# Merging the key split of the second attention, moving its weights to the queries, copying a query half on GpSimd, and four more embedding buffers

## The chip, the core and the metric

The kernel runs as one program on one core of a Trainium2 chip. The metric is the device time of one execution in microseconds; the time of a kernel is the median of its runs.

The engines, as the profile names them: PE is TensorE (matrix products; PEld is its loading of the stationary operand), DVE is VectorE, ACT is ScalarE, POOL is GpSimd, and SP is the engine that only issues DMAs here.

## What is computed

One encoder layer for two sequences (prompt and sample) of 2048 tokens and 1024 features. It normalises, projects, runs two attentions beside each other, gates each, projects back and adds; then it adds an embedding product under a second gate:

```python
h = rms_norm(x, norm_w)
q_a, k_a, v_a, g_a, q_b, k_b, v_b, g_b = jnp.split(h @ w_in, IN_SPLITS, axis=-1)
...
o_a = windowed_gqa_sink(q_a, k_a, v_a, sink_a) * jax.nn.silu(g_a)
q_b = rms_norm(q_b.reshape(b, s, B_HEADS, HEAD_DIM), q_norm_b)
k_b = rms_norm(k_b.reshape(b, s, B_HEADS, HEAD_DIM), k_norm_b)
v_b = v_b.reshape(b, s, B_HEADS, HEAD_DIM)
o_b = neighbourhood_attn(q_b, k_b, v_b, rpb_b) * jax.nn.silu(g_b)
x = x + jnp.concatenate([o_a, o_b], axis=-1) @ w_out
return x + (p @ w_ple) * jax.nn.sigmoid(x @ w_ple_gate)
```

`neighbourhood_attn` sees the tokens as a grid of 32 rows by 64 columns; a query looks at 8 rows by 16 columns of keys, with a learned bias, over 8 heads of 64 features. A score is the sum over the 64 features of query times key, so the product of the two norm weights and the scale 1/8 may stand on either side of it.

## The kernel before, in words

**Stages.** The first attention (A) with its projections comes first, until about 600 us. The second attention (B) follows, until about 1590 us. Then come three large matrix products, each done in seven products of half-size blocks (L1134). This document is about B and the turn from B to the products.

**How B is tiled.** It runs in two halves of four heads each. In a half, each sequence has 16 tiles of 128 tokens (8 grid rows by 16 grid columns), so there are 32 tiles a half and 64 in all. The first half also projects the values of all eight heads; the second has less to project. A tile f goes through `proj_b` (L705): split the input into a high and a low part, project (`project`, L451), take the root of the mean square on GpSimd, normalise keys and queries, and store keys and values. Seven tiles later its queries are used: `prep_q` (L573) and `unit_b` (L788) make the scores, `softmax` (L615), transposes, values and output of the same tile. So the last seven units run with no projection beside them.

**High and low parts.** Every operand of a matrix product is held as two numbers: a high part (rounded to the format that TensorE multiplies) and the remainder. ACT writes the high part from the PSUM bank, then DVE writes the difference.

**Keys.** TensorE transposes the four normalised key heads of a tile into one PSUM bank (L735): two pairs of heads side by side, in each pair one head in partitions 0 to 63 and one in 64 to 127. Before the change the loops at L737 and L738 go over the two pairs i and the two heads e. Each of the four turns has one ACT instruction `k1` (L745, high part, scaled by the weights `wk`) and one DVE instruction `k2` (L749, low part). They store into `big[0]` for the first pair and `big[1]` for the second. The store is strided: the key buffer runs by grid row and then grid column, and the instruction takes a tile's elements by column and then row. In the profile these instructions are "ACTIVATE big<-bank,wk" and "SCALAR_TENSOR_TENSOR big<-bank,wk,big".

**Queries.** For each of the two heads e of a pair, `prep_q` has an ACT copy of the high part (`o1`, L602), a DVE subtraction for the low part (`o2`, L604), and a DMA (`o3`, L607) that copies the high part into the other 64 partitions, since a score matmul multiplies one 128-partition stationary operand by keys that hold high and low parts in the two halves of the partitions. All of it is 64 partitions by 256 elements in B.

**Embeddings.** `embed` (L909) multiplies the embedding input by its weights in 64 groups of six matmuls with 512 columns. A group takes a PSUM bank and an `ev` buffer, ACT evicts it into the buffer (L929), and a DMA stores it to memory (`ple_d`). The buffers become free for that when the projections have ended (`no_projections`, L1018): two of the eight `wb` weight tiles give four buffers. All groups must be done before the second of the seven products, whose weights take the place of the embedding weights.

**What sets the order.** The program is recorded by a planner (`Flow`, L93). Each `op` carries an engine, an assumed duration in ns, its inputs, a priority (the lower number goes first) and the buffers it takes and frees. The planner runs these assumed times forward and writes each engine's instructions in the order that comes out; on the chip every engine then takes its instructions in that order. Embeddings have the priority 5003.5 on TensorE, so they fill what attention leaves. GpSimd's sums of weights (`combine`, L887) fill in the same way. A change of an assumed duration or an engine can therefore move instructions far from it.

Of the kernel before, what the change touches and what calls it, by code (L numbers as in the profile page):

```python
# [12 lines left out]
F32 = mybir.dt.float32  # L13
F32R = mybir.dt.float32r
# [209 lines left out]
def emit(ctx, tc, io):  # L224
# [57 lines left out]
    op = F.op  # L282
# [65 lines left out]
    big = [new([128, 4096], F32R, f"big{i}") for i in range(3)]  # L348
# [3 lines left out]
    ks_b = [big[i].rearrange("p (e r c) -> p e r c", e=2, c=64) for i in range(2)]  # L352
# [220 lines left out]
    def prep_q(f):  # L573
# [26 lines left out]
        for e in range(2):  # L600
            a, z = 64 * e, 64 - 64 * e
            o1 = op("ACT", 92 + 0.78 * w, lambda e=e, a=a: A.copy(dst_of(hi[e]()[a:a + 64]), src_of(a)), [t, first_hi], pr,  # L602
                    take=[q1[e]] if in_a else [q1[0]] if e == 0 else (), free=[bank])
            o2 = op("DVE", 85 + 1.04 * w, lambda e=e, a=a: V.tensor_tensor(  # L604
                out=dst_of(q2.t[a:a + 64, e, :w]), in0=src_of(a), in1=dst_of(hi[e]()[a:a + 64].bitcast(F32)), op=ALU.subtract),
                [o1, *out[:1]], pr, take=[q2] if e == 0 else (), free=[bank])
            o3 = dma(lambda e=e, z=z: hi[e]()[z:z + 64].bitcast(F32), lambda e=e, a=a: hi[e]()[a:a + 64].bitcast(F32), w / 4, [o1], pr)  # L607
# [97 lines left out]
    def proj_b(f, w_qk, qk_done, w_v, v_done, prios, gate):  # L705
# [31 lines left out]
        for i in range(2):  # L737
            for e in range(2):  # L738
                a, z = 64 * e, 64 - 64 * e

                def hl(i=i, e=e, a=a, z=z):
                    src = kb.t[a:a + 64, 128 * i:128 * i + 128].rearrange("p (c r) -> p c r", r=8)
                    return (src, *(ks_b[i][p:p + 64, e, 8 * b:8 * b + 8, 16 * cb:16 * cb + 16].rearrange("p r c -> p c r") for p in (a, z)))

                def k1(v=hl, a=a):  # L745
                    src, hi, _ = v()
                    A.activation(hi, src, AF.Copy, scale=wk[a:a + 64, 1:2])

                def k2(v=hl, a=a):  # L749
                    src, hi, lo = v()  # L750
# [3 lines left out]
                keys_of[f] += [o1, o2]  # L754
# [263 lines left out]
    def no_projections():  # L1018
# [275 lines left out]
```

## Time and profile before

| | |
|---|---|
| median of 3 runs | 2567.73 us (2567.34 to 2568.16) |
| the profiled execution's own time | 2568.98 us |
| its span, first to last instruction | 2566.9 us |
| mean granted TensorE clock | 0.985 |
| PE, DVE, ACT, POOL busy in the span | 96%, 69%, 61%, 46% |

The prediction quotes rows in these forms. A row of busy time has the stretch, its length, and for each engine the busy us and the number of instructions. A row of a group has the source line, engine, operation, output<-inputs, shape and count, then the busy us and the mean ns of one, then the idle time ahead of these instructions and what ended it. L215 is the helper that records every operation, so groups are told apart by the names of their buffers: `big` holds keys in both attentions, `q` the split queries, `s` scores, `p_t` probabilities, `xr` split input, `ev` embedding results, `misc` small work. A row of waits has who waited for whom, the total in us, how often, and the longest. L276 is a matrix product, L279 a transpose, L1134 one of the three large products.

### The profile page before, as it was taken

The numbers are of one execution on the slowest core, as the hardware profiler recorded it, in microseconds if no ns is written. First come the engines' busy times: TensorE is split into PE (matmuls) and PEld (weight loads), VectorE is DVE, ScalarE is ACT, GpSimd is POOL, SyncE is SP. The second block draws the span as 40 slices with busy tenths as digits, with TensorE's granted clock in tenths as the row PEclk, the third lists the DMA queues.
The fourth block names the chain that finished last, engine by engine and source line by source line (L and its number), as shares of the span: only waits on it lengthen the run. The fifth ranks groups of instructions, "written<-read, shape, count | busy, mean of one in ns | idle before, by whom it ended". The sixth has DMA issues, their size and how long they took to land. (4 is left out here: it accounts for less than half of the span.)

```text
span 2566.9 us, 39582 instructions
## 1 busy us (share of the span) xinstructions
PE 2462.5 (96%) x12468; PEld 2042.7 (80%) x12468; DVE 1769.5 (69%) x3622; ACT 1569.9 (61%) x3430; POOL 1169.9 (46%) x1537
## 2 busy tenths in 40 slices
PE   8999999999999999998989989899999999999999
PEld 6888888888787877777767778788888788888887
DVE  5888888884657565677776773477678566766765
ACT  6889889885657566677777786544443222344443
POOL 6677777765454554466666553043332000013323
PEclk9999999999999999999999999999999999999999
DMA  5634363336667666666766567866567556646654
GB/s 161 189 112 148 115 184 106 92 103 216 214 216 219 213 209 210 217 189 186 226 202 206 185 208 243 273 205 204 187 230 266 191 199 206 228 146 220 201 177 139
DMA packets 267345, 490.20 MB, mean 191 GB/s; under 512 B 28832, under 2 KB 91488, under 8 KB 257632
## 3 DMA queue, kind: packets, MB, share of 16 engines
q1 hardware_dynamic: 267136, 487.67, 59.8%
q8 instruction: 99, 1.62, 0.3%
q14 instruction: 110, 0.90, 0.1%
HBM read 340.73 MB, written 145.78 MB: 190 GB/s over the span
## 5 line engine op out<-in xcount | busy, mean ns | idle before, releaser
L276 PE MATMUL bank<-wb,xr 128*128 128x512 f32 x1536 | 399.9, 405 | 7.7 <-DVE big L215 3.1
L276 PE MATMUL bank<-wa,xr 128*128 128x512 f32 x1536 | 391.3, 400 | 6.0 <-ACT wa L215 2.9
L215 POOL TENSOR_TENSOR xr<-st,xr 128x512 fp32r<-128x512 f32 x208 | 269.4, 1297 | 225.3 <-ACT xr L215 214.7
L276 PEld LDWEIGHTS bank<-wb,xr 128*128 128x128 f32 x1536 | 285.6, 193 | 68.1 <-DVE big L215 3.8
L215 ACT ACTIVATE s<-s,nm 128x288 f32<-128x288 f32 (+6 forms) x512 | 290.0, 567 | 76.6 <-DVE nm L215 70.4
L276 PEld LDWEIGHTS bank<-wa,xr 128*128 128x128 f32 x1536 | 281.4, 190 | 63.8 <-ACT wa L215 3.6
L215 POOL TENSOR_SCALAR s<-s,rd 128x288 f32<-128x288 f32 (+6 forms) x512 | 270.4, 546 | 123.4 <-DVE rd L215 97.2
L215 DVE TENSOR_TENSOR p_t<-bank,p_t 128x512 fp32r<-128x512 f32 (+3 forms) x440 | 262.1, 625 | 52.9 <-ACT p_t L215 48.8
L215 ACT CAST p_t<-bank 128x512 fp32r<-128x512 f32 (+3 forms) x440 | 221.7, 542 | 47.1 <-PE bank L279 40.5
L279 PE MATMUL bank<-ident,s 128*128 128x128 f32 (+2 forms) x1568 | 221.2, 276 | 28.4 <-DVE big L215 12.0
L276 PE MATMUL bank<-big,q 128*128 128x288 f32 (+4 forms) x1024 | 226.7, 338 | 18.5 <-DVE p_t L215 6.2
L279 PEld LDWEIGHTS bank<-ident,s 128*128 128x128 f32 (+2 forms) x1568 | 180.1, 139 | 58.7 <-issue 10.3
L1134 PE MATMUL bank<-o,wa 128*128 128x512 f32 x912 | 209.8, 389 | 0.0
L276 PEld LDWEIGHTS bank<-big,q 128*128 128x128 f32 x1024 | 160.2, 191 | 57.3 <-DVE p_t L215 15.9
L215 DVE SCALAR_TENSOR_TENSOR big<-bank,wk,big 64x128 fp32r<-64x128 f32 x320 | 137.1, 429 | 99.2 <-ACT big L215 91.6
L215 POOL TENSOR_TENSOR s<-s,q 128x512 f32<-128x512 f32 x20 | 32.2, 1614 | 376.3 <-DVE s L215 375.6
L1134 PEld LDWEIGHTS bank<-o,wa 128*128 128x128 f32 x912 | 171.2, 188 | 35.5
L1134 PE MATMUL bank<-xr,wa 128*128 128x512 f32 x816 | 189.7, 392 | 4.2 <-ACT wa L215 2.3
L215 DVE TENSOR_TENSOR misc<-bank,misc 64x256 f32<-64x256 f32 (+1 forms) x256 | 141.8, 554 | 73.9 <-ACT misc L215 69.3
L215 POOL TENSOR_TENSOR y<-vr,half_neg 128x8 f32<-128x8 f32 (+1 forms) x128 | 185.5, 1449 | 8.7
L215 ACT COPY misc<-bank 64x256 f32<-64x256 f32 (+1 forms) x256 | 121.1, 473 | 103.4 <-PE bank L276 89.6
L1134 PEld LDWEIGHTS bank<-xr,wa 128*128 128x128 f32 x816 | 154.3, 189 | 37.1 <-ACT wa L215 2.8
(182 smaller groups left out, 4790.1 us busy)
## 6 DMA issues: line engine op xcount, KB each, us to landing
st<-x_b SPq DMA_DIRECT2D x128, 256.0 KB
vw<-v_d SPq DMA_DIRECT2D x101, 256.0 KB
st<-x_a SPq DMA_DIRECT2D x64, 256.0 KB
st<-x_n SPq DMA_DIRECT2D x64, 256.0 KB
v_d<-sq SPq DMA_DIRECT2D x64, 256.0 KB
ple_d<-ev SPq DMA_DIRECT2D x64, 256.0 KB
st<-ple_d SPq DMA_DIRECT2D x64, 256.0 KB
v_d<-sq SPq DMA_DIRECT2D x96, 128.0 KB
```

Source lines behind the costliest of these rows:

```text
L215: return lambda *a, **k: self.tc.keep_in_program_order(f(*a, **k))
L276: pinned(nc.tensor.matmul(out, lhsT, rhs, start=start, stop=stop))
L279: pinned(nc.tensor.transpose(out, in_, ident[:in_.shape[0], :in_.shape[0]]))
L1134: pinned(nc.tensor.matmul(st[0].t, w[k][:, x, c:c + 128], o[y][:, k], start=first and k == 0 and j == 0, stop=k == 3 and j == 2, skip_grou ...
```

## The change

1. The two key buffers become the two halves of one tile, `pair`. `k1` and `k2` now cover both pairs of heads: two instructions of each kind per tile of 64 partitions by 256 elements, where there were four of 64 by 128. They no longer apply weights. The durations assumed are 560 and 540 ns, where 398 and 375 stood.
2. The weights go to the queries of B: the ACT copy becomes an ACT scaling (`ACTIVATE q<-bank,wk`), the DVE subtraction a scaled subtraction (`SCALAR_TENSOR_TENSOR`). In the first attention nothing changes.
3. In B the copy of the high half into the other partitions is no DMA on SP's queue any more, but a GpSimd copy of 64x256, assumed at 480 ns. These are 128 instructions.
4. Four `wb` tiles instead of two become embedding buffers: eight buffers for four.

```diff
-    big = [new([128, 4096], F32R, f"big{i}") for i in range(3)]
+    pair = new([128, 2, 4096], F32R, "pair")
+    big = [pair[:, 0], pair[:, 1], new([128, 4096], F32R, "big2")]
...
-    ks_b = [big[i].rearrange("p (e r c) -> p e r c", e=2, c=64) for i in range(2)]
+    ks_b = pair.rearrange("p i (e r c) -> p i e r c", e=2, c=64)
...
+            def high(e=e, a=a):
+                if in_a:
+                    A.copy(dst_of(hi[e]()[a:a + 64]), src_of(a))
+                else:
+                    A.activation(hi[e]()[a:a + 64], src_of(a), AF.Copy, scale=wk[a:a + 64, 1:2])
+
+            def rest(e=e, a=a):
+                out, high = dst_of(q2.t[a:a + 64, e, :w]), dst_of(hi[e]()[a:a + 64].bitcast(F32))
+                if in_a:
+                    V.tensor_tensor(out=out, in0=src_of(a), in1=high, op=ALU.subtract)
+                else:
+                    V.scalar_tensor_tensor(out=out, in0=src_of(a), scalar=wk[a:a + 64, 1:2], in1=high, op0=ALU.mult, op1=ALU.subtract)
...
-            o3 = dma(lambda e=e, z=z: hi[e]()[z:z + 64].bitcast(F32), lambda e=e, a=a: hi[e]()[a:a + 64].bitcast(F32), w / 4, [o1], pr)
+            if in_a:
+                o3 = dma(lambda e=e, z=z: hi[e]()[z:z + 64].bitcast(F32), lambda e=e, a=a: hi[e]()[a:a + 64].bitcast(F32), w / 4, [o1], pr)
+            else:
+                o3 = op("POOL", 480, lambda e=e, a=a, z=z: G.tensor_copy(out=hi[e]()[z:z + 64], in_=hi[e]()[a:a + 64].bitcast(F32)), [o1], pr)
...
-        for i in range(2):
-            for e in range(2):
-                a, z = 64 * e, 64 - 64 * e
...
-                    A.activation(hi, src, AF.Copy, scale=wk[a:a + 64, 1:2])
...
-                    V.scalar_tensor_tensor(out=lo, in0=src, scalar=wk[a:a + 64, 1:2], in1=hi.bitcast(F32), op0=ALU.mult, op1=ALU.subtract)
-                o1 = op("ACT", 398, k1, [kp], pr, free=[kb])
-                o2 = op("DVE", 375, k2, [o1], pr, free=[kb])
...
+        for e in range(2):
+            a, z = 64 * e, 64 - 64 * e
+
+            def hl(e=e, a=a, z=z):
+                src = kb.t[a:a + 64, :256].rearrange("p (i c r) -> p i c r", i=2, r=8)
+                return (src, *(ks_b[p:p + 64, :, e, 8 * b:8 * b + 8, 16 * cb:16 * cb + 16].rearrange("p i r c -> p i c r") for p in (a, z)))
...
+                A.copy(hi, src)
...
+                V.tensor_tensor(out=lo, in0=src, in1=hi.bitcast(F32), op=ALU.subtract)
+            o1 = op("ACT", 560, k1, [kp], pr, free=[kb])
+            o2 = op("DVE", 540, k2, [o1], pr, free=[kb])
...
-        for j in range(2):
+        for j in range(4):
             t = new([128, 2, 512], F32, f"wb{j}", f"ev{j}")
             give(ev_pool, [t[:, 0], t[:, 1]])
```

The order in which instructions stand moves with it. The first place is ACT's queue in the second half of B, at the split of one tile's keys. Before, `big_178` and `big_179` are the two key buffers, `q_182` queries, `s` with `den` an exponential:

```order
L215 ACTIVATE big_178<-bank_159,wk 64x16x8 x2
L215 COPY misc<-bank_154 64x512
L215 CAST p_t<-bank_156 96x3x128
L215 ACTIVATE big_179<-bank_159,wk 64x16x8 x2
L215 CAST p_t<-bank_160 96x3x128
L215 CAST p_t<-bank_154 96x3x128
L215 ACTIVATE s_169,den<-s_169,nm 128x384
```

A place of the same kind in the changed program, where `pair` holds both key buffers:

```order
L215 ACTIVATE q_181<-bank_156,wk 64x256 x2
L215 ACTIVATE s_162,den<-s_162,nm 128x288
L215 CAST pair<-bank_159 64x2x16x8 x2
L215 ACTIVATE s_164,den<-s_164,nm 128x384
L215 ACTIVATE s_165,den<-s_165,nm 128x384
```

Four key instructions of a bank have become two, and the queries' copies carry `wk`.

The second place is GpSimd's queue in the second half of B. `s` with `rd` are the four divisions of a unit's softmax, `xr` the low part of a tile's input, `vr` and `y` the root. Before:

```order
L215 TENSOR_TENSOR xr_173<-st_175,xr_173 128x512
L215 TENSOR_SCALAR s_165<-s_165,rd 128x384
L215 TENSOR_SCALAR s_166<-s_166,rd 128x384
L215 TENSOR_SCALAR s_163<-s_163,rd 128x384
L215 TENSOR_SCALAR s_168<-s_168,rd 128x384
L215 TENSOR_SCALAR s_169<-s_169,rd 128x288
```

In the changed program (`CAST q_181<-q_181` is the new copy):

```order
L215 TENSOR_SCALAR s_164<-s_164,rd 128x512
L215 CAST q_181<-q_181 64x256
L215 TENSOR_SCALAR s_165<-s_165,rd 128x360
L215 TENSOR_SCALAR s_166<-s_166,rd 128x360
L215 TENSOR_SCALAR s_167<-s_167,rd 128x360
L215 TENSOR_SCALAR s_168<-s_168,rd 128x360
L215 CAST q_181<-q_181 64x256 x3
```

The copies stand between the divisions of one unit and the next.

The third place is SP's queue at the end of the embeddings. `ple_d<-ev` stores an embedding result; `big_178<-sums`, `big_179<-sums` and `a_15910<-w_g_c` load weights of the large products. Before:

```order
L215 DMA big_178<-sums_115 128x512 x3
L215 DMA ple_d_96<-ev_15031 128x512 x2
L215 DMA ple_d_96<-ev_15032 128x512 x2
L215 DMA big_178<-sums_115 128x512
L215 DMA big_179<-sums_115 128x512 x2
L215 DMA ple_d_97<-ev_15031 128x512 x2
L215 DMA ple_d_97<-ev_15032 128x512 x2
L215 DMA big_179<-sums_115 128x512 x2
```

In the changed program the stores of the last embeddings (`ple_d_98`) stand there, `pair<-sums` and `wa<-w_g_c` being loads of product weights:

```order
L215 DMA ple_d_98<-ev_14813 128x512 x2
L215 DMA ple_d_98<-ev_14814 128x512 x2
L215 DMA pair<-sums_115 128x512
L215 DMA ple_d_98<-ev_14815 128x512 x2
L215 DMA ple_d_98<-ev_14816 128x512 x2
L215 DMA pair<-sums_115 128x512 x4
L215 DMA wa_135<-w_g_c 128x512
```

All but one of the weight loads have moved behind the last store. On TensorE, 243 embedding matmuls stood before the first large product and 141 behind its first 48 matmuls; now 150 stand before it and 234 behind.

More of the change, by code (lines that the diff above doesn't have):

```diff
@@ L601, in prep_q @@
             a, z = 64 * e, 64 - 64 * e
-            o1 = op("ACT", 92 + 0.78 * w, lambda e=e, a=a: A.copy(dst_of(hi[e]()[a:a + 64]), src_of(a)), [t, first_hi], pr,
-                    take=[q1[e]] if in_a else [q1[0]] if e == 0 else (), free=[bank])
-            o2 = op("DVE", 85 + 1.04 * w, lambda e=e, a=a: V.tensor_tensor(
-                out=dst_of(q2.t[a:a + 64, e, :w]), in0=src_of(a), in1=dst_of(hi[e]()[a:a + 64].bitcast(F32)), op=ALU.subtract),
-                [o1, *out[:1]], pr, take=[q2] if e == 0 else (), free=[bank])
-            o3 = dma(lambda e=e, z=z: hi[e]()[z:z + 64].bitcast(F32), lambda e=e, a=a: hi[e]()[a:a + 64].bitcast(F32), w / 4, [o1], pr)
+            def high(e=e, a=a):
[9 more added lines that the diff above has]
+                    V.scalar_tensor_tensor(out=out, in0=src_of(a), scalar=wk[a:a + 64, 1:2], in1=high, op0=ALU.mult, op1=ALU.subtract)
+            o1 = op("ACT", 92 + 0.78 * w, high, [t, first_hi], pr,
+                    take=[q1[e]] if in_a else [q1[0]] if e == 0 else (), free=[bank])
+            o2 = op("DVE", 85 + 1.04 * w, rest, [o1, *out[:1]], pr, take=[q2] if e == 0 else (), free=[bank])
+            if in_a:
+                o3 = dma(lambda e=e, z=z: hi[e]()[z:z + 64].bitcast(F32), lambda e=e, a=a: hi[e]()[a:a + 64].bitcast(F32), w / 4, [o1], pr)
+            else:
+                o3 = op("POOL", 480, lambda e=e, a=a, z=z: G.tensor_copy(out=hi[e]()[z:z + 64], in_=hi[e]()[a:a + 64].bitcast(F32)), [o1], pr)
             out += [o2, o3]
@@ L736, in proj_b, with k1, k2 @@
         keys_of[f] = []
-        for i in range(2):
-            for e in range(2):
-                a, z = 64 * e, 64 - 64 * e
[L741 to L746, printed above, removed]
-                    A.activation(hi, src, AF.Copy, scale=wk[a:a + 64, 1:2])
-                def k2(v=hl, a=a):
-                    src, hi, lo = v()
-                    V.scalar_tensor_tensor(out=lo, in0=src, scalar=wk[a:a + 64, 1:2], in1=hi.bitcast(F32), op0=ALU.mult, op1=ALU.subtract)
-                o1 = op("ACT", 398, k1, [kp], pr, free=[kb])
-                o2 = op("DVE", 375, k2, [o1], pr, free=[kb])
-                keys_of[f] += [o1, o2]
+        for e in range(2):
[3 more added lines that the diff above has]
+                return (src, *(ks_b[p:p + 64, :, e, 8 * b:8 * b + 8, 16 * cb:16 * cb + 16].rearrange("p i r c -> p i c r") for p in (a, z)))
+            def k1(v=hl):
+                src, hi, _ = v()
+                A.copy(hi, src)
+            def k2(v=hl):
+                src, hi, lo = v()
+                V.tensor_tensor(out=lo, in0=src, in1=hi.bitcast(F32), op=ALU.subtract)
+            o1 = op("ACT", 560, k1, [kp], pr, free=[kb])
+            o2 = op("DVE", 540, k2, [o1], pr, free=[kb])
+            keys_of[f] += [o1, o2]
         after_pe[f] = (ops[-1], ops[-1])
@@ L813, in sc @@
                 mm(bank.t[:, :n].rearrange("p (r c) -> p r c", c=ncol), w[:, 128 * (h // 2):128 * (h // 2) + 128],
-                   ks_b[h // 2][:, h % 2, r0:r0 + nr, c0:c0 + ncol], x == 0, x == 1)
+                   ks_b[:, h // 2, h % 2, r0:r0 + nr, c0:c0 + ncol], x == 0, x == 1)
         kd = [o for g in need for o in keys_of[g]]
```

## The prediction

> **What bounds the kernel now.** I read the page first, then busy time by stage, then who waited for whom in the stages that the change touches, then the groups by shape for prices.
>
> Busy time in four stretches (start:end, length, then busy us of PE, PEld, DVE, ACT and POOL, each with its count; granted clock, DMA share, GB/s): second attention while values are still projected, second attention with less projection, its last seven units, and the turn into the three products. The fifth row is a stretch of pure products.
>
> ```profile
> 625.00:1108.00 483.00, 457.55 (x2339) 373.05 (x2338) 295.39 (x736) 303.09 (x705) 242.55 (x279) 0.99 0.69 214
> 1108.00:1495.00 387.00, 350.79 (x1815) 278.61 (x1814) 281.79 (x696) 287.96 (x669) 247.26 (x283) 0.95 0.63 199
> 1495.00:1587.00 92.00, 87.40 (x478) 72.74 (x477) 52.86 (x136) 72.26 (x166) 37.99 (x51) 0.98 0.72 225
> 1587.00:1660.00 73.00, 64.95 (x274) 52.37 (x273) 25.76 (x24) 38.35 (x64) 6.75 (x5) 0.95 0.87 292
> 2000.00:2200.00 200.00, 200.00 (x884) 165.68 (x883) 126.27 (x125) 48.05 (x42) 0.00 (x0) 1.00 0.61 207
> ```
>
> TensorE's work is the same after the change (12468 matmuls), so only its idle time can go: 25.5 us in the first row, 36.2 in the second, 4.6 in the third, 8.1 in the fourth. No other engine is full: in the second row ACT is busy 74%, DVE 73%, POOL 64%. Whatever the change frees on them counts only as far as TensorE waits for it. Whom it waits for, in each half of the stage (engine and line, waited for: us in total, times, longest):
>
> ```profile
> PE bank L279 <- DVE big L215: 8.2, 6, 3.0
> ```
>
> ```profile
> PE bank L276 <- DVE p_t L215: 6.3, 11, 1.2
> PE bank L276 <- DVE big L215: 5.2, 5, 2.4
> PE bank L279 <- DVE big L215: 4.5, 6, 1.4
> ...
> PE bank L279 <- POOL s L215: 1.9, 3, 1.0
> ```
>
> The first row is the first half (640 to 1080 us), the others the second (1080 to 1600). The largest single cause is "DVE big", the key split: 8.2 + 5.2 + 4.5 = 17.9 us. GpSimd's softmax division costs only 1.9.
>
> **The change part by part.** Prices of the key and query steps, by shape (count | busy us, mean ns | idle before); the last two rows are the same key step in the first attention, where its output lies without a stride:
>
> ```profile
> L215 ACT ACTIVATE big<-bank,wk 64x128 fp32r<-64x128 f32 x232 | 112.5, 485 | 39.3 <-PE bank L279 33.9 <-DVE qb L215 1.1 <-DVE misc L215 1.0
> L215 DVE SCALAR_TENSOR_TENSOR big<-bank,wk,big 64x128 fp32r<-64x128 f32 x232 | 103.9, 448 | 82.4 <-ACT big L215 78.1 <-PE bank L279 1.0
> L215 DVE TENSOR_TENSOR q<-bank,q 64x256 fp32r<-64x256 f32 x122 | 51.1, 419 | 1.8
> L215 ACT CAST q<-bank 64x256 fp32r<-64x256 f32 x118 | 42.8, 364 | 3.9 <-PE bank L276 1.1 <-PE bank L279 1.1
> L215 DVE TENSOR_TENSOR qb<-bank,y 128x256 f32<-128x256 f32 x57 | 23.5, 412 | 0.0
> L215 DVE SCALAR_TENSOR_TENSOR sq<-bank,rs_b,sq 128x256 fp32r<-128x256 f32 x50 | 22.9, 477 | 11.2 <-ACT sq L215 10.9
> L215 ACT ACTIVATE sq<-bank,rs_b 128x256 fp32r<-128x256 f32 x50 | 21.8, 473 | 15.4 <-PE bank L276 11.5 <-issue 2.7 <-DMA v_d<-sq 0.8
> ```
>
> ```profile
> L215 ACT ACTIVATE big<-bank,wk 64x128 fp32r<-64x128 f32 x60 | 21.7, 362 | 3.8 <-PE bank L279 3.2
> L215 DVE SCALAR_TENSOR_TENSOR big<-bank,wk,big 64x128 fp32r<-64x128 f32 x60 | 21.0, 350 | 7.0 <-ACT big L215 4.1 <-PE bank L279 1.4
> ```
>
> *Keys.* The strided store adds 485 - 362 = 123 ns on ACT and 448 - 350 = 98 on DVE for 128 elements. The merged instruction stores 256 strided elements and has no weight to apply, so it starts from the plain query rows, 364 and 419 ns. If the stride costs by instruction, it takes 487 and 517 ns; if by element, 364 + 2 x 123 = 610 and 419 + 2 x 98 = 615. I take the second, the dearer, because a doubled run doubles what is done per element. Per tile ACT gives 4 x 485 - 2 x 610 = 720 ns back, DVE 4 x 448 - 2 x 615 = 562.
> [...]
>
> *Queries.* Each half of a query tile changes from a plain copy to a scaled one: 473 - 364 = 109 ns more on ACT, 477 - 412 = 65 on DVE, twice per unit. Net per tile and unit: ACT 720 - 218 = 502 ns less, DVE 562 - 130 = 432 less; over 64, 32.1 us of ACT and 27.6 of DVE, half of each in either half of the stage. (Stride by instruction: 48 and 40.)
>
> *The copied half.* 128 DMAs leave SP's queue, 128 copies of 64x256 enter GpSimd's. The trace has no such copy; nearest are these rows. The last one is of SP's own waits in the second half:
>
> ```profile
> L215 POOL TENSOR_TENSOR misc<-misc 128x256 f32<-128x256 f32 x64 | 47.7, 745 | 131.8 <-DVE misc L215 111.8 <-issue 9.5 <-PE bank L276 8.1
> L215 POOL TENSOR_SCALAR s<-s,rd 128x512 f32<-128x512 f32 x64 | 43.2, 693 | 23.6 <-DVE rd L215 21.9 <-PE bank L276 1.6
> L215 POOL TENSOR_SCALAR s<-s,rd 128x288 f32<-128x288 f32 x60 | 29.2, 506 | 15.0 <-DVE rd L215 15.0
> ```
>
> ```profile
> SPq L215 <- ACT q L215: 27.4, 16, 3.7
> ```
>
> One input costs (693 - 506) / 224 = 0.835 ns an element, so 256 come to 506 - 32 x 0.835 = 479 ns; the two-input row, 745, is the upper bound. I take 479: 61 us over the stage, 31 in the second half, where POOL goes from 247 to 278 of 387 us. Not full, so I cost it at nothing; what hides it is that TensorE waits 1.9 us for divisions. If that cover goes, it is the first rival. SP's gain is worth nothing to the end: none of TensorE's waits above is for a DMA of queries.
>
> *What reaches the end, before the last seven units.* One tile's key chain is 4 x 485 + 4 x 448 = 3.73 us now and 2 x 610 + 2 x 615 = 2.45 then, 34% shorter; of the 17.9 us waited for it that is 6.1 us, the lower bound. The upper bound is all of DVE's 27.6 us (ACT's is larger, but DVE ends most waits). Between, by half: the first has TensorE at 95%, so I take 4 us; in the second, with 36.2 us idle, 11 of DVE's 13.8. Together 15 us.
>
> *The last seven units and the turn.* Embedding groups (six matmuls of 512 columns, one ACT copy, one store) fill TensorE there. More buffers would let more of them in, but the order shows the reverse: between the last projection and the last values 201 of their matmuls stood, now 96; before the first product 243, now 150; the other 234 follow it. A matmul of 512 columns takes 200 / 884 = 0.226 us (fifth stretch row), so 105 x 0.226 = 23.7 us of TensorE's work leaves the third stretch. ACT loses 17 evictions and 6 splits of embedding input there, 6 key instructions net:
>
> ```profile
> L215 ACT ACTIVATE ev<-bank 128x512 f32<-128x512 f32 x48 | 28.3, 596 | 15.3 <-PE bank L276 11.7 <-ACT p_t L215 1.6 <-ACT xr L215 0.9
> L215 ACT CAST xr<-st 128x512 fp32r<-128x512 f32 x126 | 77.6, 619 | 11.0 <-PE bank L276 6.8 <-DMA st<-x_b 3.2
> ```
>
> That is 17 x 0.596 + 6 x 0.619 + (8 x 0.485 - 2 x 0.610) - 6 x 0.109 = 15.9 us of 72.3. If the stretch keeps ACT's share (72.3 of 92, 79%), it shrinks to 56.4 / 0.785 = 72 us, by 20; TensorE then does the 23.7 us later at full rate: 3.7 us lost. If it keeps TensorE's share (95%), (87.4 - 23.7) / 0.95 = 67: 1.3 won. If it does not shrink at all, 23.7 lost. I take 3.7 lost.
>
> The turn now (start us, us, engine, work, idle before):
>
> ```profile
> 1606.96 26.68 PE L276 MATMUL bank<-xr,wa 128*128 128x512 f32 x117
> 1634.46 5.80 PE L276 MATMUL bank<-xr,wa 128*128 128x512 f32 x24 [0.82 <-ACT ev L215]
> 1646.33 1.22 PE L1134 MATMUL bank<-xr,big 128*128 128x512 f32 x2 [6.06 <-ACT xr L215]
> 1648.71 9.70 PE L1134 MATMUL bank<-xr,big 128*128 128x512 f32 x34 [1.16 <-DVE xr L215]
> ```
>
> A piece of the chain that ended last, from the middle of that burst (start us, us, what):
>
> ```profile
> 1624.51 0.48 issue
> 1624.99 0.60 ACT ev L215
> 1625.60 0.32 SPq L215
> 1625.92 0.05 issue
> 1625.97 4.67 DMA big<-sums
> ```
>
> Stores of embeddings and loads of product weights alternate on SP, and ACT alternates with them: an eviction stands behind the cast of a weight, which waits 4.67 us for its load, which stands behind the stores of earlier evictions. With eight buffers the order has nearly all those loads behind the last store, so the burst runs through, but the weights of the next product arrive after it: 0.7 us of stores, 4.7 of loads, 0.62 + 0.69 of split, against the 6.06 + 1.16 now. I take 1 us won (bounds: 6 won, 4 lost).
>
> Sum: -15 + 3.7 - 1 = -12.3 us. The profiled execution took 2568.98 us (span 2566.9 and 2.1 around it), 1.25 over the median 2567.73; 2568.98 - 12.3 - 1.25 = 2555.4, so 2555.
>
> **The rivals.** *GpSimd's queue inherits SP's wait.* SP waited 27.4 us in the second half for ACT's query copies, harmlessly. Now GpSimd waits for them, and behind the copies stand the next unit's four divisions, for which TensorE's transposes wait, as the order shows. If all 27.4 reach TensorE, the time is 2555 + 27 = 2582; it is slower than before once more than 12 + 5 of the 27.4 do. For it: GpSimd takes its instructions in order and is the engine that gains work. Against: the divisions themselves wait for ACT's exponentials, so part of the wait is there anyway. [...] I give 0.17.
> *TensorE's idle is not ACT's or DVE's length* but hand-over between engines, which fewer instructions leave as it is: only the 6.1 us of key waits go, the last stretch gives 3.7 back, the turn 1: 3 us won, 2564. For it: neither engine is over 74%. 0.16.
> *The last seven units do not shrink* because two units in flight set their pace and not ACT: -15 + 23.7 - 1 = 8 slower, 2575. For it: DVE is busy only 53 of 92 us there. Against: with ACT at 79%, evictions do stand in its way. 0.07.
> That the merged key tile makes a key write wait for reads of the other pair can be set aside: in the order with its waits, the new key instructions wait for their own transposes or for DVE, none for a score matmul. A merged instruction could undo its gain only above 970 ns on ACT, twice the present row.
>
> **How the numbers follow.** Forecast 0.60, rivals 0.17, 0.16, 0.07. A measurement of this kernel can tell 0.2%, 5.1 us, from no change. Faster by more than that: the forecast and a little of the second rival, 0.62; within: the rest of the second and the weak end of the first, 0.17; slower: 0.21. The forecast's own low end is 15 replaced by 27.6, so 2543, and 5 more if the turn's six go: 2538. Upwards the range takes in the second and third rivals and half of the first: 2577.
>
> **What would show it.** In the changed profile: merged key rows near 610 and 615 ns; scaled query rows near 473 and 484; the copies near 479; waits of TensorE for the key split down from 17.9 us by a third or more; POOL waits of TensorE still a few us; the last seven units near 72 us; one burst of some 234 embedding matmuls without a gap, then one gap of 6 to 9 us. Wrong would be: TensorE waits for "POOL s" of 10 us or more (first rival), second-half idle still near 36 us (second), the last units still near 92 us (third).

## The result, and the profile after

| | before | changed |
|---|---|---|
| median of 4 runs each | 2567.53 us | 2525.14 us (2524.61 to 2528.1) |
| the profiled execution's own time | 2568.98 us | 2524.61 us |
| its span | 2566.9 us | 2522.7 us |
| mean granted TensorE clock | 0.985 | 0.991 |

The ratio is 0.984, with a 95% interval from 0.9823 to 0.9857: the change gains 42 us where 12 were forecast. The sign and most prices were right; the whole gain was three to four times the forecast.

Busy time by stage. The stages are cut at the same events in both traces: the first projection of the second attention's first half, the first and the last projection of its second half, the last product with values, and the end of the second of the large products. Before, the first two of these stretches (the other two stand in the prediction, 1495 to 1587 and 1587 to 1660, a us short of the event):

```profile
542.00:1088.00 546.00, 522.16 (x2644) 426.26 (x2643) 331.84 (x823) 339.78 (x791) 277.99 (x316) 0.99 0.66 206
1088.00:1495.00 407.00, 369.03 (x1918) 294.18 (x1917) 294.96 (x735) 302.76 (x706) 258.19 (x297) 0.95 0.63 198
```

The same four stretches of the changed kernel:

```profile
542.00:1066.00 524.00, 512.50 (x2641) 423.25 (x2640) 318.04 (x757) 323.68 (x726) 302.57 (x376) 0.99 0.66 208
1066.00:1460.00 394.00, 359.12 (x1935) 288.94 (x1935) 289.14 (x685) 294.75 (x656) 284.50 (x363) 0.98 0.62 198
1460.00:1522.00 62.00, 60.06 (x359) 50.27 (x359) 47.51 (x123) 54.71 (x131) 31.39 (x48) 1.00 0.65 201
1522.00:1618.00 96.00, 91.06 (x383) 73.65 (x382) 23.34 (x21) 51.45 (x82) 12.93 (x12) 0.95 0.71 245
```

The first half became 22 us shorter (4 forecast), the second 13 (11 forecast), and the last seven units with the turn went from 166 to 158 us (2.7 us of loss forecast). In the first half TensorE does the same matmuls (the counts differ by where the cut falls), yet its busy time fell by 9.7 us beside 12.3 us of idle time. In the second half its busy time fell by 9.9 us and its idle time by only 3.1 (38.0 to 34.9), while the granted clock rose from 0.95 to 0.98.

TensorE's waits for the key split in the changed kernel, first half (one row) and second (two rows), and its waits for GpSimd's divisions in the second half (the last two rows):

```profile
PE bank L276 <- DVE pair L215: 0.7, 1, 0.7
```

```profile
PE bank L279 <- DVE pair L215: 3.1, 3, 1.4
PE bank L276 <- DVE pair L215: 2.4, 3, 1.6
PE bank L279 <- POOL s L215: 0.9, 1, 0.9
PE bank L276 <- POOL s L215: 0.3, 1, 0.3
```

The 17.9 us have become 6.2. Waits for other work of DVE grew meanwhile: in the second half those for `nm` from 6.4 to 10.7 us and those for `misc` from 5.4 to 8.1. The prices of the new instructions, from the groups by shape between 625 and 1460 us:

```profile
L215 DVE TENSOR_TENSOR pair<-bank,pair 64x256 fp32r<-64x256 f32 x116 | 72.0, 621 | 55.7 <-ACT pair L215 54.3
L215 ACT CAST pair<-bank 64x256 fp32r<-64x256 f32 x116 | 71.1, 613 | 39.4 <-PE bank L279 38.0
L215 DVE SCALAR_TENSOR_TENSOR q<-bank,wk,q 64x256 fp32r<-64x256 f32 x114 | 54.8, 481 | 1.7
L215 ACT ACTIVATE q<-bank,wk 64x256 fp32r<-64x256 f32 x114 | 52.8, 466 | 3.1 <-PE bank L279 0.7 <-PE bank L276 0.4
L215 POOL CAST q<-q 64x256 fp32r<-64x256 f32 x114 | 45.0, 395 | 27.7 <-ACT q L215 17.9 <-issue 3.9
```

The forecast prices were 615, 610, 484, 473 and 479. And TensorE's timeline at the turn:

```profile
1544.62 53.20 PE L276 MATMUL bank<-xr,wa 128*128 128x512 f32 x234
1600.87 1.22 PE L1148 MATMUL bank<-xr,pair 128*128 128x512 f32 x2 [3.04 <-ACT xr L215]
1603.25 0.80 PE L1148 MATMUL bank<-xr,pair 128*128 128x512 f32 x1 [1.16 <-DVE xr L215]
1604.78 8.13 PE L1148 MATMUL bank<-xr,pair 128*128 128x512 f32 x21 [0.74 <-ACT pair L215]
```

One unbroken burst of 234 embedding matmuls, then gaps of 4.9 us in all.

### The profile page after: what moved, and what is told of

Its sections match the earlier page's. It is cut to its first block, busy times and chain, and to the rows that moved or that the text cites. A ratio compares the mean times of both kernels' runs of the same rounds, so it can differ in the third digit from the quotient of the medians.

```text
span 2522.7 us, 39235 instructions
## 1 busy us (share of the span) xinstructions
PE 2440.8 (97%) x12468; PEld 2032.5 (81%) x12468; DVE 1748.6 (69%) x3494; ACT 1541.1 (61%) x3302; POOL 1219.2 (48%) x1665
## 4 chain that ended last, share of the span: by engine, by line
PE 82%; DVE 8%; ACT 5%; POOL 3%; issue 2%; DMA 1%; SPq 0%; POOLq 0%; DVEq 0%; ACTq 0%
PE bank L276 39%; PE bank L1148 36%; PE bank L279 6%; DVE s L215 2%; ACT s L215 2%; DVE p_t L215 2%; DVE misc L215 1%; DVE pair L215 1%; POOL s L215 1%; POOL y L215 1%; ACT pair L215 1%; ACT p_t L215 1%; DVE ssq L215 1%; ACT misc L215 0%; DVE q L215 0%
## 5 line engine op out<-in xcount | busy, mean ns | idle before, releaser
L276 PEld LDWEIGHTS bank<-wb,xr 128*128 128x128 f32 x1536 | 278.3, 189 | 62.7 <-DVE p_t L215 3.4
L276 PE MATMUL bank<-pair,q 128*128 128x288 f32 (+4 forms) x1024 | 225.0, 335 | 18.0 <-DVE nm L215 9.9
L276 PEld LDWEIGHTS bank<-pair,q 128*128 128x128 f32 x1024 | 158.3, 190 | 54.3 <-DVE nm L215 23.4
L215 POOL TENSOR_TENSOR s<-s,st 128x512 f32<-128x512 f32 x47 | 78.4, 1676 | 200.0 <-ACT s L215 125.6
```

The costliest lines, as they stand in the source:

```text
L215: return lambda *a, **k: self.tc.keep_in_program_order(f(*a, **k))
L276: pinned(nc.tensor.matmul(out, lhsT, rhs, start=start, stop=stop))
```

## The experiments

Eighteen kernels, e1 to e18, in the order in which they ran. Each was measured beside the kernel before on the same chip (its median there was 2567.2 to 2569.0 us). Times are medians, with the ratio to before and its 95% interval.

**Which of the edits it is.** First each edit by itself. Merged keys with the weights on the queries, alone (from the changed kernel):

```diff
-                o3 = op("POOL", 480, ... G.tensor_copy(...), [o1], pr)
+                o3 = dma(..., w / 4, [o1], pr)
...
-        for j in range(4):
+        for j in range(2):
```

> Only the merged key split with the weights on the queries; query halves still copied by DMA, four embedding buffers. Key theory (the shorter key split on ACT and DVE brings most of the 42 us): 25 to 40 us faster than before. Copy theory (the copies leaving SP's queue bring most): under 15 us faster. Buffer theory: under 15 us faster.

e1: 2529.87 us, 0.9853 (0.9837 to 0.9869). The copies alone (from before):

```diff
-            o3 = dma(..., w / 4, [o1], pr)
+            o3 = dma(...) if in_a else op("POOL", 480, ... G.tensor_copy(...), [o1], pr)
```

> Only the copy of the query half by GpSimd in the second attention; keys split as before. Key theory: within 8 us of before, or slower by what GpSimd's 61 us add. Copy theory: 20 us or more faster. First rival of the prediction (GpSimd holds up the divisions): slower than before by 10 us or more.

e2: 2574.79 us, 1.0028 (1.0017 to 1.0038): alone they lose 7 us. The buffers alone (from before):

```diff
-        for j in range(2):
+        for j in range(4):
```

> Only eight embedding buffers for four. The order puts all 384 embedding matmuls before the first large product, where 243 stood. Key theory: at most 8 us either way. Buffer theory: 15 us or more faster, all of it after the last projection.

e3: 2565.57 us, 0.9994 (0.9984 to 1.0003): nothing. Merger and buffers, without the copies:

```diff
-                o3 = op("POOL", 480, ... G.tensor_copy(...), [o1], pr)
+                o3 = dma(..., w / 4, [o1], pr)
```

> The change without the GpSimd copy: merged keys, weights on queries, eight buffers, queries still copied by DMA. Key theory: the same as the changed kernel within 8 us, 35 to 45 us faster than before. Copy theory: at most half of the 42 us. If the parts only add up: the sum of what the merge alone and the buffers alone give.

e4: 2528.68 us, 0.9852 (0.9837 to 0.9867), as without the buffers. So the key step, with the order that the planner draws for it, makes 38 of the 42 us.

**Shorter instructions, or another order?** The merger shortens the step on the chip, and it also makes the planner draw up another order. The next two kernels take one without the other. The changed order with the old instructions:

```diff
-                A.copy(hi, src)
+                for i in range(2):
+                    A.activation(hi[:, i], src[:, i], AF.Copy, scale=wk[a:a + 64, 1:2])
...
-                V.tensor_tensor(out=lo, in0=src, in1=hi.bitcast(F32), op=ALU.subtract)
+                for i in range(2):
+                    V.scalar_tensor_tensor(out=lo[:, i], in0=src[:, i], scalar=wk[a:a + 64, 1:2], in1=hi[:, i].bitcast(F32), op0=ALU.mult, op1=ALU.subtract)
```

> The changed program's order, place for place on TensorE and GpSimd (copies on GpSimd and eight buffers too), but at each place of a merged key instruction stand the two old ones of 64x128 with the weights on them, and the queries are plain. Length theory (the gain is the key step's shorter time on the chip: 4 x 485 + 4 x 448 = 3.73 us a tile before, 2 x 615 + 2 x 622 = 2.47 after): the gain is lost, about 2565 us (2560 to 2575). Order theory (the gain is the other order that the planner draws up when it reckons with fewer and shorter key instructions): the gain stays, about 2530 us (2525 to 2538). In between, both have a share, in proportion.

e5: 2542.31 us, 0.9902 (0.9887 to 0.9917). The old order with the new instructions:

```diff
-                def k1(v=hl, a=a):
-                    src, hi, _ = v()
-                    A.activation(hi, src, AF.Copy, scale=wk[a:a + 64, 1:2])
+                def k1(v=hl, i=i):
+                    if i == 1:
+                        src, hi, _ = v()
+                        A.copy(hi, src)
```

(the same for `k2`, the key views and the queries as in the change)

> The order of before, place for place on TensorE and GpSimd, with the merged key instructions at the place of the second pair's and nothing at the first pair's; weights on the queries; DMA copies and four buffers as before. Length theory: most of the 38 us that the merger alone gave, 2530 to 2540 us. Order theory: no gain, about 2567 us (2560 to 2575).

e6: 2539.12 us, 0.9888 (0.9872 to 0.9905). Each seemed to give 25 to 28 us, together 42: neither theory held alone, and what the "order" gave with the old instructions needed an explanation. Two runs asked whether the plan's assumed times matter by themselves. Before, with two numbers changed:

```diff
-                o1 = op("ACT", 398, k1, [kp], pr, free=[kb])
-                o2 = op("DVE", 375, k2, [o1], pr, free=[kb])
+                o1 = op("ACT", 485, k1, [kp], pr, free=[kb])
+                o2 = op("DVE", 448, k2, [o1], pr, free=[kb])
```

> Before, with nothing changed but the durations that the planner assumes for the four key pairs of instructions: 485 and 448 ns, as the trace of before measured them, for 398 and 375. Length theory: the instructions are the same, so within some 10 us of before, 2558 to 2575. Order theory, in the form that the old order was bad because the plan thought the key step shorter than it is: a good part of the 38 us, below 2550.

e7: 2563.49 us, 0.9983 (0.9974 to 0.9993): 4 us. The change with measured durations in the plan:

```diff
-            o1 = op("ACT", 560, k1, [kp], pr, free=[kb])
-            o2 = op("DVE", 540, k2, [o1], pr, free=[kb])
+            o1 = op("ACT", 615, k1, [kp], pr, free=[kb])
+            o2 = op("DVE", 622, k2, [o1], pr, free=[kb])
...
-                o3 = op("POOL", 480, ...
+                o3 = op("POOL", 395, ...
```

(and 469 and 483 for the two query splits of the second attention)

> The changed program with the durations assumed for its new instructions set to what its trace measured: keys 615 and 622 ns for 560 and 540, query splits 469 and 483 for 292 and 351, GpSimd copies 395 for 480. Length theory: within 6 us of the changed program, 2519 to 2531. Order theory: the better plan gives more again, below 2519.

e8: 2522.98 us, 0.982 (0.9806 to 0.9835). It is the lowest median of all, but its interval overlaps that of the changed kernel, so the two are not told apart.

**What of the order it is.** The changed order keeps a head's two pairs together, and it reckons with less time. Together alone, at the old reckoning (from before):

```diff
-        for i in range(2):
-            for e in range(2):
+        for e in range(2):
...
+            def k1(v=hl, a=a):
+                for i in range(2):
+                    src, hi, _ = v(i)
+                    A.activation(hi, src, AF.Copy, scale=wk[a:a + 64, 1:2])
...
+            o1 = op("ACT", 796, k1, [kp], pr, free=[kb])
+            o2 = op("DVE", 750, k2, [o1], pr, free=[kb])
```

> Before, with the old instructions, and the planner told to take them in two blocks instead of four: per head, ACT's two scalings of both pairs together (assumed 796 ns, twice the old 398), then DVE's two subtractions together (750). The assumed sum is as before. What made the new order worth 25 us with the old instructions: if the grouping, the first half of the second attention (545.7 us before, 530.3 with the new order) falls to about 532 and the whole to 2550 (2545 to 2556). If that the planner reckoned with a shorter key step, nothing: 2562 to 2570. If neither, but a lucky draw of the order, anywhere within 10 us of before.

e9: 2543.13 us, 0.9901 (0.9886 to 0.9916): the whole 25 us, but not where I expected them: the first half took 535 us, not 532, and most of the gain lies in the second (381.9 us for 407.6). Less time reckoned alone:

```diff
-                o1 = op("ACT", 398, k1, [kp], pr, free=[kb])
-                o2 = op("DVE", 375, k2, [o1], pr, free=[kb])
+                o1 = op("ACT", 280, k1, [kp], pr, free=[kb])
+                o2 = op("DVE", 270, k2, [o1], pr, free=[kb])
```

> Before, with nothing changed but the assumed durations of the key instructions, 280 and 270 ns for 398 and 375, so that the planner's sum for a tile is that of the merged step (2 x 560 and 2 x 540), while the chip still takes 485 and 448 each. If the shorter reckoning made the new order good: about 2550 (2545 to 2556). If the grouping did: 2562 to 2575, since the plan is further from the chip than before.

e10: 2592.31 us, 1.0094 (1.0077 to 1.0111): a plan that is too hopeful about the key step costs 24 us, more than either side of the expectation. So it was not the shorter reckoning.

**Copies and buffers in company.** The change without the buffers:

```diff
-        for j in range(4):
+        for j in range(2):
```

> The change without the four more embedding buffers. If the buffers have no share in the whole, as alone: as the changed program, 2525 (2521 to 2529). If the copies gain only with them: 2530 or more, as the merger without copies.

e11: 2534.09 us, 0.9862 (0.9847 to 0.9877): the copies bring the merger nothing by themselves (2529.87 without them). Copies and buffers together bring it 3 to 5 us (0.9853 to 0.984), which the intervals do not separate, in an order that the planner drew anew each time. The change with each copy made twice, at the same place:

```diff
-                o3 = op("POOL", 480, lambda ...: G.tensor_copy(...), [o1], pr)
+                def both(e=e, a=a, z=z):
+                    for _ in range(2):
+                        G.tensor_copy(out=hi[e]()[z:z + 64], in_=hi[e]()[a:a + 64].bitcast(F32))
+                o3 = op("POOL", 480, both, [o1], pr)
```

> The changed program in its own order, but each GpSimd copy of a query half made twice in a row: 128 x 395 ns = 50.6 us more work for GpSimd within the second attention, where it is busy 302.6 of 524 and 284.5 of 394 us. If the copies are hidden as costed: within 6 us of the changed program, 2520 to 2531. If GpSimd's queue hands its delay on to TensorE through the divisions (first rival's mechanism): 2535 or more, with TensorE's waits for divisions well above the 1.2 us of the changed program.

e12: 2536.27 us, 0.9873 (0.9858 to 0.9887): 8 us more by the ratios, 11 by the medians, but not by the rival's way. TensorE's waits for divisions in the second half stayed at 1.2 us. What grew is DVE's wait for the root of the mean square, which GpSimd computes in the same queue; that this wait is what costs the time is likely, but no run tests it. Changed kernel, then doubled copies, 1066 us to the last projection:

```profile
DVE misc L215 <- POOL y L215: 7.7, 10, 2.3
```

```profile
DVE misc L215 <- POOL y L215: 17.2, 15, 2.3
```

**One engine's step, and the copies at a fixed order.** The change, with DVE's part in two instructions:

```diff
-                V.tensor_tensor(out=lo, in0=src, in1=hi.bitcast(F32), op=ALU.subtract)
+                for i in range(2):
+                    V.tensor_tensor(out=lo[:, i], in0=src[:, i], in1=hi[:, i].bitcast(F32), op=ALU.subtract)
```

> The changed program in its own order, but DVE's part of each key step in two instructions of 64x128, back to back, without weights; ACT's stays merged. The same order with both parts in two was 2542 us, with both merged 2525. If the two engines' times count in series (ACT 94.3 to 78.5 us over the stage, DVE 102.4 to 79.4): about 2535. If TensorE only feels DVE: 2540 or more. If only ACT: 2525.

e13: 2532.56 us, 0.9867 (0.9852 to 0.9882). With ACT's part in two:

```diff
-                A.copy(hi, src)
+                for i in range(2):
+                    A.copy(hi[:, i], src[:, i])
```

> The counterpart: ACT's part in two instructions of 64x128, back to back, without weights; DVE's stays merged. In series: about 2532. DVE alone counts: 2525. ACT alone counts: 2540 or more.

e14: 2527.21 us, 0.9846 (0.9831 to 0.9861): not told apart from the change. My premise for the two was wrong: ACT's part in two did not take 94.3 us over the stage. First ACT in two instructions, then ACT merged (changed kernel), 542 to 1520 us:

```profile
L215 ACT CAST pair<-bank 64x128 fp32r<-64x128 f32 x256 | 78.5, 408 | 46.1 <-PE bank L279 44.7
```

```profile
L215 ACT CAST pair<-bank 64x256 fp32r<-64x256 f32 x128 | 78.5, 613 | 46.2 <-PE bank L279 44.8
```

256 instructions of 408 ns make 104 us, but the engine was busy for 78.5: neighbours overlap, so that two plain instructions back to back cost what the merged one costs. Busy time is a union; a sum of durations is not. The change with the copies as DMAs, at the same places of the order:

```diff
-                o3 = op("POOL", 480, lambda ...: G.tensor_copy(...), [o1], pr)
+                o3 = op("POOL", 480, lambda ...: D.dma_start(...), [o1], pr)
```

> The changed program in its own order on TensorE, ACT, DVE and GpSimd, but each copy of a query half is issued as a DMA on SP's queue at that place, so GpSimd has 50.6 us less to do. If the copies are hidden as costed: within 5 us of the changed program, 2520 to 2530. If GpSimd's work costs as the doubling showed (11 us for 50.6): about 2514. If the DMA lands too late for the scores: 2530 or more.

e15: 2523.65 us, 0.9828 (0.9811 to 0.9844): no difference from the change. The change with the plan told the measured key and query durations and without the copies:

```diff
-                o3 = op("POOL", 395, lambda ...: G.tensor_copy(...), [o1], pr)
+                o3 = dma(..., w / 4, [o1], pr)
```

> The changed program without the GpSimd copies (DMA as before), with the durations assumed for the key and query instructions set to those measured; the planner draws its own order. If the copies cost the change some 10 us: about 2513. If they are free, as the run with the measured plan and copies: 2523 (2518 to 2528).

e16: 2536.33 us, 0.9879 (0.9864 to 0.9893): 13 us worse than with the copies, against both expectations. At a fixed order the copies cost nothing, so this is the order that the planner drew.

**The partitions.** Overlap was the new thing to look for. Before, one tile's key step on ACT, then on DVE:

```profile
1203.69 1.93 ACT L215 ACTIVATE big<-bank,wk 64x128 fp32r<-64x128 f32 x4
```

```profile
1205.79 1.80 DVE L215 SCALAR_TENSOR_TENSOR big<-bank,wk,big 64x128 fp32r<-64x128 f32 x4
```

Four times 485 is 1.94: no overlap, though the four follow each other. In the grouped run four ACT instructions took 1.50 us. The start times show why: a neighbour that works on the same 64 partitions starts 0.28 us after, one that changes to the other 64 starts 0.47 us after. The old loops had the heads inside and changed partitions at every instruction. The last two kernels separate this from the grouping. Before, with the loops exchanged and the order as it was:

```diff
-        for i in range(2):
-            for e in range(2):
+        for e in range(2):
+            for i in range(2):
```

> Before, with only the two loops over the key step exchanged: heads outside, pairs inside, so that the four instructions go over partitions 0-63, 0-63, 64-127, 64-127 and not 0-63, 64-127, 0-63, 64-127. Same instructions, same assumed durations, the same order place for place. If neighbours on the same partitions overlap and those that change partitions do not: ACT's busy time for them falls from 124.1 us toward 94 and DVE's from 114.7 toward 102, as in the grouped run, and the time to about 2545 (2540 to 2552). If the planner's grouping was it: 2562 to 2572.

e17: 2540.08 us, 0.9883 (0.9868 to 0.9897). The grouped order with alternating partitions:

```diff
-        for e in range(2):
+        for i in range(2):
...
-                for i in range(2):
-                    src, hi, _ = v(i)
-                    A.activation(hi, src, AF.Copy, scale=wk[a:a + 64, 1:2])
+                for e in range(2):
+                    src, hi, _ = v(e)
+                    A.activation(hi, src, AF.Copy, scale=wk[64 * e:64 * e + 64, 1:2])
```

(`k2` alike)

> The grouped run with its planned blocks and its order place for place, but each block takes the two heads of one pair (partitions 0-63, then 64-127) and not the two pairs of one head. If the change of partitions costs: ACT 124 and DVE 115 us again, and the time 2558 or more. If the grouping was it: 2543 as the grouped run (2538 to 2548).

e18: 2566.4 us, 0.9987 (0.9977 to 0.9997). With the exchanged loops the same two steps read:

```profile
1185.21 1.47 ACT L215 ACTIVATE big<-bank,wk 64x128 fp32r<-64x128 f32 x4
```

```profile
1187.31 1.59 DVE L215 SCALAR_TENSOR_TENSOR big<-bank,wk,big 64x128 fp32r<-64x128 f32 x4
```

ACT's part took 124.2 us over the stage and DVE's 114.6, as before. The times of both orders, with and without the change of partitions:

| | partitions alternate | neighbours on the same partitions |
|---|---|---|
| order of before | 1 (before) | 0.9883, 0.9868 to 0.9897 (e17) |
| grouped order | 0.9987, 0.9977 to 0.9997 (e18) | 0.9901, 0.9886 to 0.9916 (e9) |

In us of 2567.5, going from the left column to the right is worth 30 and 22, going down a row 3 won or 5 lost. So the change of partitions costs 22 to 30 us in either order, and the grouping nothing that shows in the total. By stage, from the starts of the same matmuls in each trace (us; the last column is how long the granted clock stood at half in the second half, see the last section):

| | first half | second half | from the last projection to the end of the second product | at half clock |
|---|---|---|---|---|
| before | 545.7 | 407.6 | 165.9 | 37.5 |
| loops exchanged (e17) | 534.0 | 390.8 | 167.8 | 13.7 |
| grouped, alternating (e18) | 545.1 | 392.7 | 177.3 | 10.2 |
| grouped (e9) | 535.4 | 381.9 | 176.4 | 3.4 |
| changed order, old instructions (e5) | 530.3 | 405.1 | 157.5 | 20.5 |
| changed | 524.4 | 393.6 | 158.5 | 13.7 |

The partitions are worth 10 to 12 us in the first half and 11 to 17 in the second, in both orders. The order does move time, though: the grouped one wins 9 to 15 us in the second half and loses 9 to 11 behind it. The changed order with the old instructions (e5) has its neighbours on the same partitions too, but its 25 us lie elsewhere (15, 2 and 8 us), so that its total equals that of e9 is partly chance. With that my first reading of e5 and e9 falls. The busy time of the step from 542 to 1520 us, in the groups by shape: before, loops exchanged (e17), DVE in two plain instructions (e13), changed.

```profile
L215 ACT ACTIVATE big<-bank,wk 64x128 fp32r<-64x128 f32 x256 | 124.1, 485 | 46.2 <-PE bank L279 40.6 <-DVE qb L215 1.1 <-DVE misc L215 1.0
L215 DVE SCALAR_TENSOR_TENSOR big<-bank,wk,big 64x128 fp32r<-64x128 f32 x256 | 114.7, 448 | 91.8 <-ACT big L215 87.2 <-PE bank L279 1.0
```

```profile
L215 DVE SCALAR_TENSOR_TENSOR big<-bank,wk,big 64x128 fp32r<-64x128 f32 x256 | 104.3, 447 | 69.9 <-ACT big L215 66.1 <-PE bank L276 1.6
L215 ACT ACTIVATE big<-bank,wk 64x128 fp32r<-64x128 f32 x256 | 97.3, 471 | 44.7 <-PE bank L279 41.6 <-DVE qb L215 1.1 <-DVE misc L215 0.4
```

```profile
L215 DVE TENSOR_TENSOR pair<-bank,pair 64x128 fp32r<-64x128 f32 x256 | 87.0, 385 | 64.8 <-ACT pair L215 63.4
```

```profile
L215 DVE TENSOR_TENSOR pair<-bank,pair 64x256 fp32r<-64x256 f32 x128 | 79.4, 621 | 65.0 <-ACT pair L215 63.4
```

The 42 us can then be put down in three steps along the kernels measured. Neighbours on the same partitions, with the changed order in it: 25 (e5; 22 and 30 at a fixed order). The weights off the keys: from e5 to e13, 0.9902 to 0.9867 or 9 us, with ACT's merger in it, which e14 shows to be worth nothing that could be measured. DVE's merger: from e13 to the change, 0.9867 to 0.984 or 7 us, but the two intervals touch, so this step is likely and not shown. The last two steps together, 17 us at the same order place for place, are shown (e5 against the change). In the order of before the merged instructions (e6, 0.9888) are not told apart from the loop exchange (e17, 0.9883); but e6 also puts the first pair's split off to the place of the second pair's, so what the merger adds there stays open. Copies and buffers: nothing of their own at a fixed order (e15 for the copies); which order the planner draws with or without them moves the time by up to 13 us (e4, e8, e11, e16), and which instruction does it there stays open.

## Why the prediction was wrong, point by point

**The prices were right, but for the copies.** Keys 613 and 621 ns (610 and 615), queries 466 and 481 (473 and 484), copies 395 (479, and so below both bounds that the rows gave). Over the stage ACT's key step fell by 124.1 - 78.5 = 45.6 us, DVE's by 114.7 - 79.4 = 35.3; the forecast had 64 x 0.720 = 46.1 and 64 x 0.562 = 36.0. The merged instruction took what a stride paid by element comes to: 613 ns on ACT, not 487, and 621 on DVE, not 517. Until then this was the author's estimate, since the strided key stores in the trace of before have one length. But the reason given for the price of before was incomplete: the 4 x 485 that the merger removes hold a loss between neighbours, which exchanging two loops removes as well (ACT's four took 1.93 us before and 1.47 in e17).

**The step that failed is "what reaches the end".** It turned 32.1 us of ACT and 27.6 of DVE into 15 us; the last projection came 35.4 us earlier (1495.2 to 1459.8). That is more than the 27.6 us that it took for the upper bound. Three sentences carried it.

*"So only its idle time can go."* Both halves show the fault: 9.7 us of the first half's gain and 9.9 of the second's are TensorE's busy time, at the same work (the counts differ by where the cuts fall). A row of the changed kernel's page gives one reason:

```profile
L276 PE MATMUL bank<-wb,xr 128*128 128x512 f32 x1536 | 396.2, 400 | 5.2 <-DVE pair L215 1.5
```

One such matmul is recorded with 400 ns, but they start 226 ns apart (200 us for 884, in the prediction). So a wait below some 174 ns lies under the record of the matmul ahead, and each longer one shows that much too short; this is an estimate from these two rows. If every matmul of the first half started at the lower quartile of its kind's distance in that trace, they would need some 485 us of the 545.7: some 60 us could go, not the idle time of some 24. In the changed kernel the same reckoning leaves some 39 us. (A kind is the same operands and shape; other ways to sort them move both figures by some 5 us.)

The busy time also hangs on the granted clock, which the forecast left out: neighbouring matmuls of projections start 427 ns apart at half clock and 229 ns otherwise (before, last section). In the second half of before TensorE was granted half its clock for 37.5 us, in the changed kernel for 13.7. By the same reckoning, an estimate that holds the waits within them too, the matmuls of these stretches started 18.5 us late in all before and 7.4 after: 11 of the 14 us that the second half gained between the starts of its projections. So it is luck that the 13 us measured there lie near the 11 forecast: only 3.1 us of idle time went where 11 were to go.

*"The first has TensorE at 95%, so I take 4 us."* It is the same fault, and a wrong size besides: 12.3 us of idle time went there, three times the 4. That half gave 21 us. In the loop exchange, with the old order and the old instructions, it gave 545.7 - 534.0 = 11.7.

*"The upper bound is all of DVE's 27.6 us (ACT's is larger, but DVE ends most waits)."* For one tile ACT's and DVE's instructions run one after the other, so the sum of both is nearer the bound: 32.1 + 27.6 = 59.7. The loop exchange took 124.1 - 97.3 = 26.8 us from ACT and 10.4 from DVE, 37 together, and its last projection came 30 us earlier; the change took some 59 and gave 35.4 there. That is 0.6 to 0.8 of the sum; I had taken 0.25. That the sum of both engines counts is argued from this, and no run shortened ACT's part alone. DVE's wait for ACT ahead of this step, which the forecast did not count at all, fell too (87.2 to 63.4 us).

**The last seven units** took 62 us (72 forecast): with 105 matmuls or 23.7 us of embedding work moved out, they became 30 us shorter, and the turn with it 22 longer (74 to 96 us). I kept ACT's share of 79%; it rose to 54.71 / 62 = 88%, so the share did not hold, and the case with TensorE's share kept (67 us) was nearer. For both together the 2.7 us of loss became a gain of some 8. From the last projection to the end of the second product e5 takes 157 us as the change does (158), e17 takes 168: this part goes with the order, not with the instructions.

**The turn** went as forecast in kind: one burst, then 4.9 us of gaps against 7.2 before (6 to 9 forecast).

**The rivals.** *GpSimd's queue inherits SP's wait*: no. GpSimd did wait 17.9 us for ACT's query halves (625 to 1460 us), but TensorE 1.2 for divisions in the second half; doubled copies cost 8 to 11 us, likely through the root, so the cover holds for one copy but not for two. *TensorE's idle is hand-over, left as it is*: its sign appeared, but not its time. The idle time of the second half stayed at 34.9 us ("near 36"): the waits for keys fell from 17.9 to 6.2 us over both halves, but those for `nm` and `misc` grew. The time is not near 2564, for the first half's idle time halved (23.8 to 11.5 us), and in the second half the gain came as busy time. *The last units do not shrink*: no, 62 us.

## What to carry to other kernels

Look at the union of busy time beside the sum of durations: where neighbours on an engine do not overlap although they follow each other, see whether they change partitions (worth 22 to 30 us here), and exchange the loops before rewriting the instructions. Where one tile passes through two engines in turn, count what both get shorter, and do not take TensorE's recorded idle time for all that it can gain. Where a planner sets the order, an edit that moves the order without cost or gain of its own still moved the time by up to 13 us here, and two changed assumptions in the plan alone by 24 (e10), so a difference of that size needs a run at a fixed order before it is put down to the edit.

## What the runs showed of the hardware that was not expected

Distances between the starts of two key instructions that follow each other directly, median, from the start times of the traces:

| | same 64 partitions | other 64 partitions |
|---|---|---|
| ACT, scaled, 64x128 (485 ns) | 283 ns (e9 128 times, e17 115) | 470 ns (e17), 491 to 499 (before) |
| DVE, scaled subtraction (448 ns) | 358 ns (e9 128, e17 111) | 451 ns (e17), 451 to 469 (before) |
| ACT, plain, 64x128 (408 ns) | 181 ns (e14 128) | 444 ns (e14) |
| DVE, plain subtraction (385 ns) | 298 ns (e13 128) | 386 ns (e13) |

On the same partitions two ACT neighbours overlap by 485 - 283 = 202 ns (plain ones by 408 - 181 = 227), two DVE neighbours by 448 - 358 = 90 (plain ones by 385 - 298 = 87). Across the two halves the starts lie about as far apart as one instruction is long: 470 to 499 ns on ACT for 485, 451 to 469 on DVE for 448, plain ones 444 for 408 and 386 for 385. No run shows the cause.

A GpSimd copy of 64x256 between the halves of the partitions took 395 ns, less than the 479 worked out from divisions.

The granted clock is not low evenly: between 500 and 1700 us of these traces it is full or half, and half in stretches of 3.4, 6.8 or 10.2 us. Six matmuls of a projection in before, first at half clock (0.50 from 1406.7 to 1409.9 us), then at full:

```profile
1406.56 2.87 PE L276 MATMUL bank<-wb,xr 128*128 128x512 f32 x6
1427.90 1.54 PE L276 MATMUL bank<-wb,xr 128*128 128x512 f32 x6
```

In that trace neighbouring matmuls of projections of 512 columns start 427 ns apart at half clock (median of 44) and 229 ns apart otherwise. Each of its nine stretches at half clock in the second half follows on 0.9 to 2.5 us of TensorE's idle time within the 3.4 us ahead (the mean over the half is 0.3). The other runs show the same difference in their mean clock (0.984 to 0.987 before, 0.991 to 0.993 changed). That shorter waits paid twice, once as idle time and once through the clock, is the author's estimate from these counts. No run varies the clock by itself, so whether the waits lower it, and how much of the gain it made, stays open.
